# Where the weight sums are issued, and which tiles come last, in a two-block fp32 trunk on one core

## The chip, the core and the metric

The kernel runs on one core of a Trainium2 chip. The metric is device time in microseconds (us), from the first to the last instruction of one launch with a small overhead around it. The kernel before was timed three times: 2754.55 us median, 2754.36 to 2760.89.

## The reference, cut to what matters

A trunk of two blocks over 512 positions of width 2048, all in fp32. The first block has two layers. Each is a normalisation, an input product, two kinds of attention with gates, and an output product that is added to x:

```
for l in range(DEPTH):                     # DEPTH = 2
    h = rmsnorm(x, attn_norm_g[l])
    proj = h @ w_in[l]
    ...                                    # ya: windowed attention, yb: latent attention, both gated
    x = x + jnp.concatenate([ya, yb], axis=-1) @ w_out[l]
x = rmsnorm(x, final_norm_g)
```

The second block puts 16 meta tokens in front, and is one layer more of that form (with stick-breaking attention and a pooling branch), with its own normalisation ahead of it and one behind it:

```
zin = h @ w_in                             # h = rmsnorm_2(hs, gain)
...
merged = sigmoid(m_attn) * (o_attn @ w_attn_up) + sigmoid(m_pool) * (o_pool @ w_pool_up)
hs = hs + merged @ w_out
```

## The kernel before

Everything is kept transposed: a tile is 128 features by 512 positions, and a tensor of width 2048 is 16 such tiles. Every fp32 operand is split into a high and a low part (ScalarE casts the high part, `...h`; VectorE subtracts it from the source, `...l`), and one product is three TensorE matmuls (high by high, low by high, high by low).

Weights come through `next_w` (L253): it takes the next entry of the list `wq`, lets SyncE (SP) load 128x1024 numbers into `wr` (three buffers), lets ScalarE cast `wh` and VectorE subtract `wl` (three buffers each), and stays two entries ahead of TensorE. A *plain* output tile takes two entries and 48 matmuls of 512 columns. A *pair* of output tiles is made in the manner of Strassen and Winograd (`run_pair`, L346): seven products of 8 x 3 matmuls of 256 columns, 168 in all, over combinations of activations (`t_set`, tiles `t12`, `t34`) and of weights (`pair_steps`, L229). Two of the weight combinations of a pair are sums of blocks of the weight matrix. They are not made on an engine but by DMA: GpSimd (POOL) issues a copy of a block into a tensor `wsd` in HBM and then a DMA that adds another block to it (`sum_step`, L224; four such DMAs per pair, 48 pairs, 192 DMAs). `next_w` issues one at three of every four weight loads, from the start of the kernel until they are used up, each held until the TensorE instruction that was last issued at that point has ended (`behind_pe`). From `wsd` SP loads them as `ws` and `wr`, and VectorE adds a further block to `ws`.

In each layer of the first block the work is, in order: the input products with attention as side work, and then the output products ("output stage"): plain tiles 0 to 3, five pairs (tiles 4 to 13), plain tiles 14 and 15. Each output tile is added to the old x (`xo`, loaded by SP), stored (`xd<-xo`, SP), squared by ScalarE (`xq`), and the square is added up by GpSimd in `SumSq` (L445). In the second layer a copy scaled with the gain of the last normalisation (`xg`) is squared and added up as well (`xgq`). The next stage's activations are the new x times a gain, stored by ScalarE as `hrd` (or `xrd`) and read back by SP as `rr` tiles, which are split into `hh` and `hl`: rows 0 to 7 in the program under plain tile 14, rows 8 to 13 under plain tile 15; tiles 14 and 15 are split from on-chip data (`raw`). `scales` then splits the summed squares (`csh`) and TensorE sums them over the partitions (`csum`).

TensorE's order is as written; side work (attention heads, `t_build`, `scales`) is put between its products by an estimated clock. Every engine and every DMA queue runs its own list in order, so that a DMA on SP's list that waits holds all behind it.

In the second block, `o_load` (L1264) reads back a tile of the pooling branch (`ol`) and splits it (`o0h` ... `o7h`); four are issued before the last `ga` product and four behind it (`PRE`). `au_loads` (L1261) loads two tiles for each product of `au`.

Of the kernel before, what the change touches and what calls it, by code (L numbers as in the profile page):

```python
# [15 lines left out]
ALU = mybir.AluOpType  # L16
# [3 lines left out]
S = 512  # L20
NB = S // P
DM = 2048
NC = DM // P
# [15 lines left out]
NSLOT = 76  # L39
M2 = NM // 2  # L40
GPLAIN = 6
PRE = 4
EARLYT = 4
HEADS = {("ga", 0): 0, ("ga", 2): 1, ("ga", 4): 2, ("ga", 6): 3, ("pu", 1): 4, ("pu", 3): 5, ("pu", 5): 6, ("pu", 7): 7}
HN = S // 2
NPLAIN = 4
NSPILL = 8
SUMPAIRS = 48
NSIDE = 3
TP_WAIT = 4000  # L50

# [53 lines left out]
def trunk_kernel(ctx, tc, xT, w_in, w_qkv, w_out, w_in2, w_pool, w_aup, w_pup, w_out2, metaT, vec, cst, outT):  # L105
    nc = tc.nc
# [8 lines left out]
    def slot(name, dt=F32, cols=S):  # L115
        t = slots.tile([P, W], dt, tag="s", name=name)
        return t[:, :cols]
# [79 lines left out]
    def load_w_dma():  # L197
        src, n = wq.popleft()
        return w_raw(src, n), n

    wsd = tc.dram_tile([SUMPAIRS, 2, P, WCOLS + 16], F32, name="wsd")[:, :, :, :WCOLS]
    presum = deque()
    last_pe = [None, 0]

    def plan_sums(pairs):


        assert len(pairs) <= SUMPAIRS
        for p in range(0, len(pairs), 2):
# [6 lines left out]
                ops += [(wsd[k, 0], a22, 1), (wsd[k, 1], a11, 1)]  # L216
            presum.extend(ops)

    def behind_pe(ins):

        tc.add_manual_dep(ins.ins, last_pe[0].name, mybir.DependencyInfo(
            mybir.DependencyClass.Sync, mybir.DependencyReason.DATA), reason="pace")

    def sum_step():  # L224
        dst, src, add = presum.popleft()
        kw = {"accum_op": ALU.add} if add else {}
        behind_pe(nc.gpsimd.dma_start(dst, src, **kw))  # L227

    def pair_steps(p, a11, a12, a21, a22, n):  # L229

# [15 lines left out]
    def load_w_split(raw, n):  # L246
        hi = wp.tile([P, WCOLS], F32R, tag="wh", name="wh")[:, :n]
        lo = wp.tile([P, WCOLS], F32R, tag="wl", name="wl")[:, :n]
        nc.scalar.copy(hi, raw)  # L249
        tt(lo, raw, f32(hi), ALU.subtract)  # L250
        wready.append((hi, lo))

    def next_w():  # L253
        while len(wready) < 2 and wq:
            if callable(wq[0][0]):
                make, n = wq.popleft()
                load_w_split(make(), n)
            else:
                load_w_split(*load_w_dma())
            last_pe[1] += 1  # L260
            if last_pe[1] > 12 and last_pe[1] % 4 and presum:
                sum_step()
        return wready.popleft()

    def gemm(nt, nu, nk, rhs, wide=False, cols=S):
# [40 lines left out]
    def tick():  # L306
        for e in side[:NSIDE]:
            if e[1] <= clock[0]:
                step(e)
# [7 lines left out]
    def run_gemm(nu, nk, rhs, wide=False, group=1, n=S):  # L317
        g = gemm(group, nu, nk, rhs, wide, n)
        while True:
            try:  # L320
                next(g)
            except StopIteration as e:
                return e.value if wide or group > 1 else e.value[0]
            tick()
# [65 lines left out]
    def load(src, name, n=S, queue=nc.sync):  # L390
        t = slot(name, F32, n)
        queue.dma_start(t, src)
        return t
# [49 lines left out]
        return ps  # L443

    class SumSq:  # L445
        def __init__(self, name, cols=S):
            self.acc = None
            self.name = name
            self.cols = cols

        def add(self, x, n=None):
            q = slot(self.name + "q", F32, self.cols)
            act(q, x, AF.Square)
            if self.acc is None:
                self.acc = q
            else:
                nc.gpsimd.tensor_tensor(self.acc, self.acc, q, ALU.add)

    def gate_sigmoid(g, name):
        a = slot(name + "a")  # L460
# [285 lines left out]
    def plan():  # L746
        pairs = []
        for lay in range(DEPTH):
            t = 0
            for kind, i in SEQ1:  # L750
                if kind == "pa":
                    wq.append((w_qkv[lay, i, :, 0:1024], 1024))
                elif kind == "pb":
                    wq.append((w_qkv[lay, i, :, 1024:1664], 640))
                elif kind == "pc":
                    wq.append((w_qkv[lay, i, :, 1664:2176], 512))
                elif kind == "cq":
                    if i == 0:
                        grouped(w_in[lay], 0, GRP)
                    t += 1  # L760
                else:
                    for u in range(2):
                        wq.append((w_in[lay, t, u], WCOLS))
                    t += 1
            grouped(w_out[lay], 0, GRP)
            w = w_out[lay]
            for j in range(GRP, NPLAIN):
                for u in range(2):
                    wq.append((w[j, u], WCOLS))
            for j in range(NPLAIN, NC - 2, 2):  # L770
                blocks = (w[j, 0], w[j, 1], w[j + 1, 0], w[j + 1, 1])
                wq.extend(pair_steps(len(pairs), *blocks, WCOLS))
                pairs.append(blocks)
            for j in range(NC - 2, NC):
                for u in range(2):
                    wq.append((w[j, u], WCOLS))
        t = 0
        for kind, i in SEQ2:
            if kind == "pw":
                wq.append((w_pool[i], 512))  # L780
            elif kind == "au":
                wq.append((w_aup[i], WCOLS))
            elif kind == "pu":
                wq.append((w_pup[i], WCOLS))
            elif not _plain(kind, i):
                if i % 2 == 0:
                    blocks = (w_in2[t, 0], w_in2[t, 1], w_in2[t + 1, 0], w_in2[t + 1, 1])
                    wq.extend(pair_steps(len(pairs), *blocks, WCOLS))
                    pairs.append(blocks)
                t += 1  # L790
            else:
                for u in range(2):
                    wq.append((w_in2[t, u], WCOLS))
                t += 1
        grouped(w_out2, 0, GRP)
        for j in range(GRP, NPLAIN):
            for u in range(2):
                wq.append((w_out2[j, u], WCOLS))
        for j in range(NPLAIN, NC - 2, 2):
            blocks = (w_out2[j, 0], w_out2[j, 1], w_out2[j + 1, 0], w_out2[j + 1, 1])  # L800
            wq.extend(pair_steps(len(pairs), *blocks, WCOLS))
            pairs.append(blocks)
        for j in [NC - 2, NC - 1] * 2:
            for u in range(2):
                wq.append((w_out2[j, u], WCOLS))
        plan_sums(pairs)

    plan()

    k2 = {}  # L810
# [14 lines left out]
    def layer(lay, h, rd, x_src, x_dst):  # L825
# [62 lines left out]
            elif kind == "ga":  # L888
                gate["a", i] = gate_silu(run_gemm(2, 8, hget), rd["r"], "ga")

        sq = SumSq("x")
        if lay == 1:
            sq2 = SumSq("xg")
        res = [None] * NC
        rawd, w = (hrd, S) if lay == 0 else (xrd, W)

# [26 lines left out]
        def plain_out(j, ps):  # L923
            xo = xos.pop(j)
            tt(xo, ps, xo, ALU.add)
            tile_done(j, xo)
# [6 lines left out]
            xo_load(j)  # L933
            plain_out(j, run_gemm(2, 8, yget))
        need(lambda: len(ts) == 8)
        for j in range(NPLAIN, NC - 2, 2):
            xo_load(j)
            xo_load(j + 1)
            c = run_pair(ts, 8)
            t0, t1 = xos.pop(j), xos.pop(j + 1)  # L940
            add_pair(c, t0, t1)
            tile_done(j, t0)
            tile_done(j + 1, t1)
        c = t0 = t1 = None
        ts = None
        for j in range(NC - 2, NC):
            xo_load(j)
            for k in (range(8) if j == NC - 2 else range(8, NC - 2)):
                res[k] = split(load(rawd[:, k, :], "rr", w), "h", w)
            plain_out(j, run_gemm(2, 8, yget))  # L950
        if lay == 0:
            load_consts1()

# [74 lines left out]
    def scale0():  # L1028
        acc = squares[0]
        for n in range(1, NC):  # L1030
            ins = nc.vector.tensor_tensor(acc, acc, squares[n], ALU.add)
            if n == 1:
                behind_pe(ins)
        squares.clear()
        parts = split(acc, "cs")
        yield 19000
        r = slot("r")
        rsqrt_of(r, colsum(parts), 1.0 / DM, S)
        rd["r"] = r
# [221 lines left out]
    def au_loads(i):  # L1261
        return load(sgd[:, i, :], "sgl"), load(ypd[:, i, :], "ypl")
# [5 lines left out]
    for kind, i in SEQ2:  # L1268
# [19 lines left out]
                nc.gpsimd.dma_start(opd[:, 2 * i + d, :], t)  # L1288
        elif kind == "pu":
            gp = load(sgd[:, NC + i, :], "sgl", queue=nc.scalar)  # L1290
            yp = slot("yp")
            tt(yp, run_gemm(1, 8, lambda c: op[c]), gp, ALU.mult)
            nc.gpsimd.dma_start(ypd[:, i, :], yp)
        elif kind == "au":
            if i == 0:
                op = None
                need(lambda: all(t is not None for t in oa))
                tset = []
                ahead = {0: au_loads(0)}
            if i + 1 < NC:  # L1300
                ahead[i + 1] = au_loads(i + 1)
            ga, yp = ahead.pop(i)
# [13 lines left out]
        elif kind == "ga":  # L1316
            if i == 0:
                tset = None
            if i == SB - 1:
                for c in range(PRE):  # L1320
                    o_load(c)
            nc.gpsimd.dma_start(gad[:, i, :], gate_silu(run_gemm(2, 8, x2), sr, "ga"))
            if i == SB - 1:
                X2 = None
                for c in range(PRE, 8):
                    o_load(c)
        elif i % 2 == 0:
# [3 lines left out]
            for d, t in enumerate(c):  # L1331
# [7 lines left out]
                else:  # L1339
                    at = i + d + (0 if kind == "ma" else NC)  # L1340
# [39 lines left out]
    for j in range(NPLAIN):  # L1380
# [3 lines left out]
        q = finish(j, first[j] if j < GRP else run_gemm(2, 8, mget), full, S)  # L1384
# [151 lines left out]
```

## Time and profile before

| | |
|---|---|
| median of three runs | 2754.55 us (2754.36 to 2760.89) |
| profiled execution, its own time | 2764.74 us |
| its span | 2762.8 us |
| TensorE clock, mean of the span | 0.972 of full |
| busy: TensorE, VectorE, ScalarE, GpSimd | 95%, 70%, 50%, 19% |
| DMA bytes by queue: SP's and ScalarE's list (q1), GpSimd's (q0) | 328.89 MB, 128.66 MB |

The stages in the trace: start up to 62 us; input stage of layer 0 up to 528; its output stage up to 742; input stage of layer 1 up to 1252; its output stage up to 1470; then the second block up to 2762.8. A row of the trace names the engine, the line of the kernel, the operation and the tiles as out<-in. Times within a stage are read from the table by windows, where PE is TensorE, DVE is VectorE, ACT is ScalarE, POOL is GpSimd; "PEclk" is the granted share of TensorE's full clock, and "DMA share" the mean busy share of the 16 DMA engines.

### The profile page before, as it was taken

The page shows a single profiled execution, that of the slowest core. Times are in us where ns is not written, and L with a number is a line of the kernel's source. Part 1 is how long each engine was busy: PE and PEld are TensorE (multiplying, and loading weights), DVE is VectorE, ACT ScalarE, POOL GpSimd, SP SyncE. Part 2 cuts the span into 40 slices and gives each one's busy share as a digit, 9 for nine tenths or more (in the row PEclk, how much of TensorE's full clock was granted, in tenths as well). Part 3 has the DMA queues.
Part 4 walks back from the last instruction along what each step waited for, and adds up shares of the span by engine and source line. Part 5 has one row for each costly group of instructions (what it writes and reads, how often), then busy time and mean ns, then how long its engine had stood idle before and what let it go on. Part 6 is the DMA issues. An engine that isn't in the chain of part 4 may idle for free.

```text
span 2762.8 us, 41611 instructions
## 1 busy us (share of the span) xinstructions
PE 2631.1 (95%) x15961; PEld 2335.1 (85%) x15961; DVE 1925.3 (70%) x2923; ACT 1389.0 (50%) x2279; POOL 535.4 (19%) x564
## 2 busy tenths in 40 slices
PE   8999999989799999998978999999999998999997
PEld 6888888788588888887966999999999986878797
DVE  7767667776367657767857778777777755675686
ACT  5445455544335445554545544335565666643353
POOL 0121233222121213232431214000000022210012
PEclk9999999999899999999988999999999998999998
DMA  5455544689664555467986754544545543566555
GB/s 182 130 149 145 140 142 137 207 250 309 210 159 134 142 153 141 130 184 223 319 255 214 217 172 157 173 154 154 167 150 170 174 131 119 174 208 209 191 172 183
DMA packets 168055, 492.52 MB, mean 178 GB/s; under 512 B 19233, under 2 KB 23841, under 8 KB 167857
## 3 DMA queue, kind: packets, MB, share of 16 engines
q1 hardware_dynamic: 113936, 328.89, 35.8%
q0 software_dynamic: 36208, 128.66, 18.9%
q10 hardware_dynamic: 17712, 32.32, 3.3%
q8 instruction: 125, 2.05, 0.3%
q14 instruction: 74, 0.60, 0.1%
HBM read 428.19 MB, written 162.27 MB: 214 GB/s over the span
## 4 chain that ended last, share of the span: by engine, by line
PE 45%; DMA 3%; DVE 3%; ACT 1%; issue 1%; POOL 0%; SPq 0%; ACTq 0%; DVEq 0%; POOLq 0%
PE mm L160 13%; PE y L160 13%; PE x L160 9%; PE z L160 8%; DMA xd<-xo 1%; DMA rr<-xrd 1%; DVE wl L129 1%; PE zB L160 1%; DVE out L1414 0%; PE so L160 0%; PE pw L160 0%; PE zA L160 0%; ACT wh L249 0%; DMA xo<-xd 0%; DMA vr<-vd 0%
## 5 line engine op out<-in xcount | busy, mean ns | idle before, releaser
L249 ACT CAST wh<-wr 128x1024 fp32r<-128x1024 f32 (+2 forms) x448 | 462.2, 1032 | 556.0 <-PE mm L160 241.9
L129 DVE TENSOR_TENSOR wl<-wr,wh 128x1024 fp32r<-128x1024 f32 (+2 forms) x448 | 564.3, 1264 | 226.8 <-ACT wh L249 212.9
L160 PE MATMUL mm<-hh,wh 128*128 128x512 f32 x1248 | 504.2, 404 | 30.2 <-ACT hh L151 23.3
L160 PE MATMUL mm<-hl,wh 128*128 128x512 f32 x1248 | 497.3, 398 | 1.4 <-DVE hl L129 0.9
L160 PE MATMUL mm<-hh,wl 128*128 128x512 f32 x1248 | 496.1, 397 | 0.6 <-DVE wl L129 0.5
L160 PEld LDWEIGHTS mm<-hh,wh 128*128 128x128 f32 x1248 | 237.6, 190 | 79.7 <-ACT hh L151 27.0
L160 PEld LDWEIGHTS mm<-hh,wl 128*128 128x128 f32 x1248 | 237.2, 190 | 56.5 <-DVE wl L129 1.7
L160 PEld LDWEIGHTS mm<-hl,wh 128*128 128x128 f32 x1248 | 237.5, 190 | 51.3 <-DVE hl L129 5.1
L249 ACT CAST wh<-ws 128x1024 fp32r<-128x1024 f32 x144 | 151.3, 1051 | 182.8 <-PE y L160 128.3
L160 PE MATMUL y<-t34h,wh 128*128 128x256 f32 (+1 forms) x768 | 217.7, 283 | 2.8 <-DVE ab L129 2.7
L160 PE MATMUL y<-t34l,wh 128*128 128x256 f32 (+1 forms) x768 | 217.1, 283 | 0.0
L160 PE MATMUL y<-t34h,wl 128*128 128x256 f32 (+1 forms) x768 | 216.5, 282 | 0.0
L129 DVE TENSOR_TENSOR wl<-ws,wh 128x1024 fp32r<-128x1024 f32 x144 | 179.3, 1245 | 24.1 <-ACT wh L249 21.3
L227 POOL DMA_DIRECT2D wsd<-in_w_in x132 | 90.8, 690 | 450.1 <-PE mm L160 219.7
L160 PE MATMUL x<-hh,wh 128*128 128x256 f32 (+1 forms) x528 | 148.9, 282 | 0.0
L160 PE MATMUL x<-hl,wh 128*128 128x256 f32 (+1 forms) x528 | 148.7, 282 | 0.0
L160 PE MATMUL x<-hh,wl 128*128 128x256 f32 (+1 forms) x528 | 148.6, 281 | 0.0
L160 PEld LDWEIGHTS y<-t34h,wh 128*128 128x128 f32 x768 | 145.3, 189 | 3.2 <-issue 3.2
L160 PEld LDWEIGHTS y<-t34l,wh 128*128 128x128 f32 x768 | 145.7, 190 | 0.0
L160 PEld LDWEIGHTS y<-t34h,wl 128*128 128x128 f32 x768 | 145.4, 189 | 0.0
L129 DVE TENSOR_TENSOR ws<-ws,wr 128x1024 f32<-128x1024 f32 x96 | 136.2, 1419 | 3.2 <-DMA wr<-in_w_out 0.2
L160 PE MATMUL z<-t12h,wh 128*128 128x256 f32 (+1 forms) x384 | 109.7, 286 | 17.8 <-ACT t12h L151 17.8
(1171 smaller groups left out, 6801.0 us busy)
## 6 DMA issues: line engine op xcount, KB each, us to landing
wr<-in_w_in SPq DMA_DIRECT2D x255, 512.0 KB, 3.9
wsd<-in_w_in POOLq DMA_DIRECT2D x132, 512.0 KB, 6.7
wr<-in_w_out SPq DMA_DIRECT2D x85, 512.0 KB, 5.3
wsd<-in_w_out POOLq DMA_DIRECT2D x60, 512.0 KB, 5.7
ws<-wsd SPq DMA_DIRECT2D x48, 512.0 KB, 4.4
wr<-wsd SPq DMA_DIRECT2D x48, 512.0 KB, 4.2
tr<-yd SPq DMA_DIRECT2D x32, 256.0 KB, 5.9
xd<-xo SPq DMA_DIRECT2D x32, 256.0 KB, 6.1
```

Source lines behind the costliest of these rows:

```text
L129: nc.vector.tensor_tensor(out, a, b, op)
L160: last_pe[0] = nc.tensor.matmul(out, a, b, start=start, stop=stop, skip_group_check=True).ins
L227: behind_pe(nc.gpsimd.dma_start(dst, src, **kw))
L249: nc.scalar.copy(hi, raw)
```

## The change

There are five edits. (1) `hold` keeps `next_w` from issuing weight sums from the start of an output stage of the first block until its last plain tile; elsewhere it issues three sums per two loads instead of three per four, each held behind a TensorE instruction three loads older (`marks[0]`). (2) The added squares `xq` and `xgq` of these stages go to VectorE. (3) Each output stage of the first block has four pairs (tiles 4 to 11) and then four plain tiles (12 to 15), with four, four, four and two rows read back under them; there are 46 pairs with sums in all. (4) All eight `o_load`s stand ahead of the last `ga` product. (5) `au_loads(0)` moves ahead of the last `pu` product. The delay of `scale0` is changed too (19000 to 23000); the order of TensorE's work is the same for it.

```diff
-PRE = 4
+PRE = 8
-SUMPAIRS = 48
+SUMPAIRS = 46
...
+    hold = [0]
+    marks = deque(maxlen=4)
...
-    def behind_pe(ins):
+    def behind_pe(ins, at=None):
-        tc.add_manual_dep(ins.ins, last_pe[0].name, mybir.DependencyInfo(
+        tc.add_manual_dep(ins.ins, (at or last_pe[0]).name, mybir.DependencyInfo(
...
-        behind_pe(nc.gpsimd.dma_start(dst, src, **kw))
+        behind_pe(nc.gpsimd.dma_start(dst, src, **kw), marks[0])
...
             last_pe[1] += 1
-            if last_pe[1] > 12 and last_pe[1] % 4 and presum:
+            marks.append(last_pe[0])
+            if last_pe[1] > 12 and hold[0] == 0 and presum:
                 sum_step()
+                if last_pe[1] % 2 and presum:
+                    sum_step()
...
-                nc.gpsimd.tensor_tensor(self.acc, self.acc, q, ALU.add)
+                self.eng.tensor_tensor(self.acc, self.acc, q, ALU.add)
...
-        sq = SumSq("x")
+        hold[0] = 1
+        sq = SumSq("x", eng=nc.vector)
         if lay == 1:
-            sq2 = SumSq("xg")
+            sq2 = SumSq("xg", eng=nc.vector)
...
-        for j in range(NPLAIN, NC - 2, 2):
+        for j in range(NPLAIN, NC - 4, 2):
             xo_load(j)
             xo_load(j + 1)
             c = run_pair(ts, 8)
...
-        for j in range(NC - 2, NC):
+        for j in range(NC - 4, NC):
             xo_load(j)
-            for k in (range(8) if j == NC - 2 else range(8, NC - 2)):
+            for k in range((j - NC + 4) * 4, min((j - NC + 5) * 4, NC - 2)):
                 res[k] = split(load(rawd[:, k, :], "rr", w), "h", w)
             plain_out(j, run_gemm(2, 8, yget))
+        hold[0] = 0
...
             gp = load(sgd[:, NC + i, :], "sgl", queue=nc.scalar)
+            if i == NC - 1:
+                ahead = {0: au_loads(0)}
```

GpSimd's list in the output stage of layer 0 (`wsd` is a weight sum, `xq` the added squares; `gag` and `ya` are a gate and an attention result of the stage ahead, `cqnsq` belongs to the stage behind). Before:

```order
L227 DMA wsd<-in_w_in 128x1024
L457 TENSOR_TENSOR xq<-xq 128x512
L227 DMA wsd<-in_w_in 128x1024 x5
L457 TENSOR_TENSOR xq<-xq 128x512 x2
L227 DMA wsd<-in_w_in 128x1024 x5
L457 TENSOR_TENSOR xq<-xq 128x512
```

Now, from the last gate of the input stage to the first work of the next one:

```order
L481 TENSOR_TENSOR gag<-gag,gaa 128x512
L612 TENSOR_TENSOR ya<-ya,gag 128x512
L850 DMA yd_91<-ya 128x512
L229 DMA wsd<-in_w_in 128x1024 x15
L463 TENSOR_TENSOR cqnsq<-cqnsq 128x512 x2
```

Sums and squares are gone from GpSimd's list between the last `yd` store and the next stage; sums begin again when its weights are loaded. Per stage the list now has 93 sums in the input stage of layer 0 and 91 in that of layer 1, and none later; before it had 48, 36 (output), 57, 35 (output) and 16 (second block).

SP's list at the end of the output stage of layer 0 (`wr` weights of the next stage, `rr` rows read back, `xo` the old x of tile 15, `xd` the store of a new x). Before:

```order
L194 DMA wr_6801<-in_w_in 128x1024
L392 DMA rr_6471<-hrd_90 128x512
L392 DMA rr_6477<-hrd_90 128x512
L194 DMA wr_6832<-in_w_in 128x1024
L392 DMA rr_6483<-hrd_90 128x512
L392 DMA xo_6563<-in_xT 128x512
L392 DMA rr_6565<-hrd_90 128x512
L194 DMA wr_6863<-in_w_in 128x1024
L899 DMA xd0_93<-xo_6563 128x512
L392 DMA rr_6571<-hrd_90 128x512
```

Now:

```order
L194 DMA wr_6715<-in_w_in 128x1024
L397 DMA rr_6415<-hrd_90 128x512
L397 DMA rr_6421<-hrd_90 128x512
L194 DMA wr_6746<-in_w_in 128x1024
L397 DMA xo_6499<-in_xT 128x512
L397 DMA rr_6501<-hrd_90 128x512
L194 DMA wr_6778<-in_w_in 128x1024
L906 DMA xd0_93<-xo_6499 128x512
L397 DMA rr_6507<-hrd_90 128x512
```

The load of the old x for tile 15 stands at the same place among the weights of the next stage; behind it two rows are still to be read back, one of them behind the store, where five more stood before.

ScalarE's list in the second block before the `au` products (`o4h` to `o7h` are the casts of pooling tiles; `vh`, `sp`, `sph` belong to the attention head that TensorE's `zA` waits for). Before:

```order
L151 CAST o3h<-ol 128x512
L151 CAST vh<-vt 128x512
L136 ACTIVATE sp<-zA 128x512
L136 ACTIVATE sp<-zB 128x512
L136 ACTIVATE sp<-sp 128x512 x4
```

Now:

```order
L151 CAST o3h<-ol 128x512
L151 CAST o4h<-ol 128x512
L151 CAST o5h<-ol 128x512
L151 CAST o6h<-ol 128x512
L151 CAST o7h<-ol 128x512
L151 CAST vh<-vt 128x512
L136 ACTIVATE sp<-zA 128x512
```

Four casts, each of which waits for its load, now stand ahead of the head's chain.

## Rows read from the trace of the kernel before

**Rows 1.** Table by windows: input and output stages of both layers
```profile
core 0: us, PE busy (x) PEld busy (x) DVE busy (x) ACT busy (x) POOL busy (x), PEclk, DMA share, GB/s
62.00:528.00 466.00, 465.56 (x2367) 391.42 (x2366) 318.03 (x614) 239.28 (x485) 110.44 (x108) 1.00 0.51 144
528.00:742.00 214.00, 172.80 (x1099) 154.17 (x1098) 132.60 (x176) 92.73 (x128) 49.61 (x53) 0.90 0.87 271
742.00:1252.00 510.00, 509.59 (x2543) 426.74 (x2544) 339.34 (x643) 254.39 (x505) 122.59 (x121) 0.99 0.53 147
1252.00:1470.00 218.00, 175.65 (x1094) 156.01 (x1093) 148.49 (x185) 102.04 (x157) 74.61 (x65) 0.88 0.85 261
```

**Rows 2.** TensorE's waits, output stage of layer 0: total, times, longest us
```profile
PE csum L160 <- ACT csh L151: 13.0, 1, 13.0
PE z L160 <- ACT t12h L151: 9.2, 2, 5.1
PE z L160 <- DVE wl L129: 6.2, 2, 4.6
PE mm L160 <- ACT hh L151: 5.2, 3, 3.6
PE mm L160 <- ACT y12h L151: 2.9, 1, 2.9
```

**Rows 3.** The same waits, output stage of layer 1
```profile
PE mm L160 <- ACT hh L151: 18.0, 3, 10.6
PE z L160 <- ACT t12h L151: 8.6, 2, 7.1
```

**Rows 4.** Table by windows: pair stretches and ends of both output stages
```profile
581.00:662.00 81.00, 74.82 (x610) 74.40 (x610) 52.54 (x62) 36.63 (x46) 22.25 (x25) 0.96 0.96 289
711.00:743.00 32.00, 12.80 (x38) 7.22 (x38) 14.74 (x20) 14.62 (x23) 3.55 (x4) 0.71 0.71 248
1300.00:1356.00 56.00, 54.94 (x458) 54.52 (x457) 44.16 (x53) 29.03 (x40) 24.38 (x22) 0.99 0.97 288
1356.00:1404.00 48.00, 41.61 (x324) 41.02 (x323) 33.66 (x39) 22.44 (x33) 20.68 (x18) 0.93 1.01 321
1428.00:1468.00 40.00, 16.53 (x42) 9.61 (x40) 17.94 (x23) 16.79 (x28) 7.12 (x6) 0.62 0.60 181
```

**Rows 5.** DMA, output stage of layer 0: GpSimd's queue, and its sums
```profile
q0 software_dynamic: 5264, 19.14, 36.7%
...
wsd<-in_w_in POOLq DMA_DIRECT2D x36, 512.0 KB, 7.7
```

**Rows 6.** DMA, input stage of layer 0: GpSimd's queue, and weight loads
```profile
q0 software_dynamic: 8112, 29.10, 27.0%
...
wr<-in_w_in SPq DMA_DIRECT2D x52, 512.0 KB, 4.1
```

**Rows 7.** Timeline, end of layer 0's output stage: start, us, engine, line, op
```profile
711.05 0.39 PE L160 MATMUL mm<-y15l,wh 128*128 128x512 f32 x1
...
711.28 0.39 PE L160 MATMUL mm<-y15h,wl 128*128 128x512 f32 x1
...
718.98 0.38 SPq L392 DMA_DIRECT2D xo<-in_xT  x1
...
735.68 3.30 ACT L151 CAST hh<-rr 128x512 fp32r<-128x512 f32 x5 [6.78 <-DMA rr<-hrd]
```

**Rows 8.** VectorE's weight add and scaled copy, by tile: ns min/median/max
```profile
L129 DVE TENSOR_TENSOR ws<-ws,wr x96: 1212/1226/2217, 557.8 to 2702.4; 128x1024 f32<-128x1024 f32 x96
...
L906 DVE TENSOR_SCALAR xg<-xo,vecs x16: 479/1515/1579, 1265.6 to 1462.7; 128x512 f32<-128x512 f32 x16
```

**Rows 9.** GpSimd's added squares, by lines: busy us, mean ns, idle before
```profile
L457 POOL TENSOR_TENSOR xq<-xq 128x512 f32<-128x512 f32 x30 | 49.9, 1664 | 89.7 <-ACT xq L136 89.7
```

**Rows 10.** Timeline, second block before the `au` products
```profile
2324.13 1.74 SPq L392 DMA_DIRECT2D ol<-opd  x4
...
2327.47 0.79 PE L160 MATMUL zA<-sph,tri 128*128 128x512 f32 x1 [4.58 <-ACT sph L151]
```

More of the change, by code (lines that the diff above doesn't have):

```diff
@@ L445, in trunk_kernel, with __init__ @@
     class SumSq:
-        def __init__(self, name, cols=S):
+        def __init__(self, name, cols=S, eng=nc.gpsimd):
             self.acc = None
+            self.eng = eng
             self.name = name
@@ L935, in layer @@
         need(lambda: len(ts) == 8)
-        for j in range(NPLAIN, NC - 2, 2):
+        for j in range(NPLAIN, NC - 4, 2):
             xo_load(j)
@@ L945, in layer @@
         ts = None
-        for j in range(NC - 2, NC):
+        for j in range(NC - 4, NC):
             xo_load(j)
-            for k in (range(8) if j == NC - 2 else range(8, NC - 2)):
+            for k in range((j - NC + 4) * 4, min((j - NC + 5) * 4, NC - 2)):
                 res[k] = split(load(rawd[:, k, :], "rr", w), "h", w)
             plain_out(j, run_gemm(2, 8, yget))
+        hold[0] = 0
         if lay == 0:
@@ L1035, in scale0 @@
         parts = split(acc, "cs")
-        yield 19000
+        yield 23000
         r = slot("r")
@@ L1298, in trunk_kernel @@
                 tset = []
-                ahead = {0: au_loads(0)}
             if i + 1 < NC:
```

## The prediction, made before the changed kernel ran

> **What bounds the kernel now.** I read the table by windows first, cut at the stage borders, to see where TensorE isn't busy. In the two input stages it lacks almost nothing: 465.56 of 466 us and 509.59 of 510, at a DMA share of 0.51 and 0.53. In the two output stages it lacks 41.2 of 214 us and 42.4 of 218, the granted clock falls to 0.90 and 0.88, and the DMA share is 0.87 and 0.85 [rows 1]. So nearly all that can be won in the first block lies in 432 us.
>
> The list of TensorE's waits says for what it waits there: in layer 0 13.0 us for `csh` (the summed squares), 9.2 for `t12h`, 6.2 for `wl`, 5.2 for `hh` (rows read back) [rows 2]; in layer 1 18.0 for `hh` and 8.6 for `t12h` [rows 3]. ScalarE and VectorE are named, but neither is full; they wait for loads: five `hh` casts come after 6.78 us of ScalarE's idleness that a DMA ended [rows 7].
>
> A finer table by windows separates two kinds of loss. In the pairs the DMA share is 0.96 to 1.01 and TensorE loses some: 81 against 74.82, 48 against 41.61, with the clock at 0.96 and 0.93. At the end of each stage it loses most: 12.80 of 32 us busy at clock 0.71, and 16.53 of 40 at 0.62 [rows 4]. In matmuls: one of 512 columns follows the last at 0.23 us (711.05 to 711.28) [rows 7], so the 38 of the first end are worth 8.7 us and the 42 of the second 9.7. Lost are 23.3 and 30.3 us, of which some is the half clock into which TensorE falls once it has stood still.
>
> **The sums and the DMA engines.** GpSimd's queue takes 36.7% of the DMA time of layer 0's output stage [rows 5], 78.5 of 214 us; nearly all of it is 36 sums, so one costs 2.18 us of all 16 engines. Without them the share there is 0.87 - 0.37 = 0.50, that of an input stage today. Layer 1's output stage has 35. Thus every load of the stage is faster, and each wait above that ends with a load shrinks.
>
> *Pairs:* idle time and lost clock come to (81 - 74.82) + 0.04 x 81 = 9.4 us in layer 0, and (56 - 54.94) + 0.01 x 56 = 1.6 and (48 - 41.61) + 0.07 x 48 = 9.8 in layer 1 [rows 4]: 20.8 together. Nothing but the full DMA engines explains it, but the 56 us stretch shows that a share of 0.97 alone costs little. I take -17; ends 0 and -21.
>
> *Start of the stages:* the waits for `t12h` are 9.2 and 8.6 us, the longest of the kind for `y12h` 2.9 [rows 2, 3]. They end with a chain (attention result, store, read back, four VectorE operations, split) of which the DMA is a part. I take -4 and -1.5; ends 0 and -21.
>
> *Input stages:* they get 45 and 34 sums more. 45 x 2.18 = 98 us lift the share of layer 0's from 0.51 to 0.72, 34 x 2.18 = 74 us that of layer 1's from 0.53 to 0.68. The cover is the three weight buffers: a load of weights is issued some 3 x 24 x 0.23 = 16.6 us less a cast and a subtraction (some 2.4) before its use, 14 us, and takes 4.1 [rows 6]. A sum took 7.7 us to land even at 0.87 [rows 5]. So I take +2; ends 0 and, at the loss of the worst stretch (9.4 of 81 us) over all 976 us, +113.
>
> The Trainium skill, "DMA: Bandwidth & Descriptors", section "Issuing engines are not separate DMA queues", speaks against the move: DMAs of all issuing engines end up on the same 16 engines and interleave, so a sum that is issued elsewhere is charged elsewhere. The trace agrees that queues share (the weight loads slow with the share); by that rule alone the gain of the pairs would turn up as a loss in the input stages, which is the slower rival below.
>
> **The ends of the stages.** Now 14 rows are read back under the last two plain tiles, eight under the first, so that most arrive after the last tile is done; TensorE then waits row by row (`hh`), and SP's list is held by weight loads whose buffers aren't free. The load of the old x for tile 15 goes out at 718.98, 7.7 us after the last matmul of that tile [rows 7]; and five more rows stand behind the store that needs it. With four rows under each of four tiles, 12 of 14 are there when tile 15 starts. But on SP's list `xo` of tile 15 still stands behind the same weight loads. With E as the end of the last plain tile: the buffer that the load ahead of `xo` needs is free at E + 2.4, `xo` lands 5 us later (between 4.1 and 7.7 [rows 5, 6]), the addition 0.65, the store and the next issue 1, the last row's load 5, then four operations (cast, square, added square, cast) of 0.66 each (3.30 for five [rows 7]): `csum` at about E + 16.7, its window 18 us instead of 32. That is -14. In layer 1 `xo` stands one weight load later on SP's list (24 x 0.23 = 5.5), and `xg` adds some 1.5: 25 instead of 40, -15. Sum -29; ends 0 (if the order on SP's list is all that counts) and -53.6, all that is lost.
>
> **Two plain tiles for a pair.** 96 matmuls of 0.23 us are 22.1 us; 168 of 256 columns at 54.94/458 = 0.120 [rows 4] are 20.2. Twice +1.9 is +4, certain within 1.
>
> **Squares on VectorE.** GpSimd makes 30 `xq` additions [rows 9]; layer 1 has 15 more for `xg`. On VectorE one is half the size of the 1.21 us `ws` addition, so some 0.65: 29 us in both stages. Against it: the `ws` addition takes 1.21 us at its best and 2.22 at its worst, `xg` 0.48 and 1.52 (median 1.515) [rows 8]; if the slow cases are those beside GpSimd's additions, 16 `ws` and 16 `xg` give back 1.0 each, 32. VectorE is at 44.16 of 56 us in the pairs of layer 1 [rows 4], so there is room either way. I take 0; ends -4 and +10, should the additions stand ahead of the `wl` that the next pair waits for.
>
> The Trainium skill, "SBUF — State Buffer", section "Who interferes with whom", says that a VectorE instruction with two SBUF inputs contends with a GpSimd instruction that reads SBUF, and that the second blocks fully. The two levels of the `ws` row agree. By this rule the edit gives the -3 above; without it VectorE would be 29 us busier, the rival below.
>
> **`o_load`s and `au_loads`.** The four later `ol` loads are issued from 2324.13 to 2325.87 [rows 10]; they wait for free tiles, which the change does not free earlier. At 4.1 us they land at 2330, and `vh` with the chain to `zA` now stands behind the cast of the last. `zA`, for which TensorE waits 4.58 us already, starts at 2327.47 [rows 10]; behind o7h's cast (2330.6) and the chain's own 4.5 us it would start near 2335, +7.7. Four casts of 0.66 are out of the way later, so +5; ends 0 (if the tiles come free earlier) and +8. `au_loads(0)` puts two loads on SP's list earlier: +1; ends 0 and +2.
>
> **The sum** is -17 - 4 - 1.5 + 2 - 29 + 4 + 0 + 5 + 1 = -39.5 us. The profiled execution took 2764.74 us, 10 above the median; the sum would make it 2725. I apply it to the median, 2754.55: 2715 us, with 2698 to 2732 as the likeliest case's own range.
>
> **Rivals.**
> - *Nearly all the loss goes:* faster loads end the stalls before the clock falls, which takes away the half clock as well. The two ends give -53, the pairs -21, half of `t12h` -9, less +9 for the other edits: -74, 2680. For it: in the input stages TensorE lacks under half a microsecond at a share of 0.51, the share that the output stages will have. Against it: SP's list, which holds `xo` of tile 15.
> - *The ends stay:* the wait is set by the order on SP's list and not by the rows, and only some -10 of the -29 come: 2734. For it: `xo` has not moved against the weights. Against it: its weight load waits for TensorE, which no longer waits for rows.
> - *VectorE becomes the bound in the pairs:* the additions cost 29 us and nothing is given back: 2744. Against it: the free and the slow `ws` addition [rows 8].
> - *The input stages fill the DMA engines (slower):* sums come in twos, weights are late, and half the loss rate of the worst stretch (5.8%) holds for 976 us: +57, 2772. It decides once a weight load takes over 14 us from issue to landing; it takes 4.1 now. Against it: 0.72 is far below 0.96.
> - *The change does not do what it says:* the output stages stay full because their own loads fill what the sums leave, 2755. Against it: the share left is 0.50.
>
> **How the numbers follow.** The forecast has 58%, the rival with the whole gain 14, the ends that stay 14, VectorE 6, the full input stages 6, no effect 2. To tell a change from none takes 0.3%, 8 us. Faster than 2746: the first three, and half of VectorE's: 88 to 89%, put at 0.88. Within 8 us: no effect and the rest of VectorE's, 0.05. Slower: 0.07, where the full input stages and a `zA` chain worse than priced lie. The range goes from 2687, into the first rival, to 2744, past the second: a little under 2 in 10 lies outside.
>
> **What would show it.** After the change the windows of the output stages should show a DMA share near 0.5 and a clock above 0.95 in the pairs; the input stages 0.68 to 0.72 with TensorE still within 2 us of full; the time from the last plain tile to `csum` near 17 and 24 us; no `ws` addition above 1.3 us in the output stages; `zA` of the last head waiting some 5 us more. The prediction is wrong if TensorE's waits for `wl` or `wh` show up in an input stage, or if the ends still take over 28 us.

## The result, and the profile after

The changed kernel takes 2714.46 us (median of four runs, 2707.63 to 2715.73) against 2756.6 in the runs beside it: a ratio of 0.984, 95% interval 0.9819 to 0.9862. It is faster by 42 us (44 by the ratio). The profiled execution took 2714.61 us, its span is 2712.5.

The table by windows, cut at the stages as they lie now (columns as in [rows 1]):

```profile
62.00:528.00 466.00, 465.86 (x2370) 391.91 (x2369) 324.68 (x621) 242.64 (x488) 141.68 (x155) 1.00 0.72 196
528.00:717.00 189.00, 166.79 (x1028) 148.99 (x1026) 123.47 (x173) 86.45 (x120) 5.56 (x8) 0.94 0.69 223
717.00:1224.00 507.00, 506.91 (x2536) 424.82 (x2537) 342.11 (x641) 254.45 (x502) 134.31 (x147) 1.00 0.64 175
1224.00:1413.00 189.00, 166.67 (x1025) 148.06 (x1023) 135.90 (x202) 99.62 (x152) 0.00 (x0) 0.94 0.61 201
```

The output stages are 25 and 29 us shorter, at a DMA share of 0.69 and 0.61 where it was 0.87 and 0.85. The input stages carry the sums now, at 0.72 and 0.64, and TensorE loses 0.1 us in either. Not all sums are gone from layer 0's output stage. Eight of the 15 that GpSimd's list has behind the last `yd` store go out there, the first at 677.04 us, 16 us ahead of the last plain tile's end: `next_w` is two loads ahead, and each sum is held only behind a TensorE instruction three loads older. From the DMA view of 528 to 717 us:

```profile
wsd<-in_w_in POOLq DMA_DIRECT2D x8, 512.0 KB, 6.6
```

GpSimd's queue has 9.1% of the DMA time of that window, for 36.7% before [rows 5]. The finer windows that answer to [rows 4]:

```profile
571.00:652.00 81.00, 81.00 (x659) 80.42 (x659) 60.34 (x78) 40.18 (x52) 0.00 (x0) 0.98 0.63 201
1268.00:1349.00 81.00, 81.00 (x664) 80.36 (x664) 65.85 (x93) 45.57 (x65) 0.00 (x0) 0.98 0.63 201
...
692.00:717.00 25.00, 9.84 (x41) 7.39 (x39) 11.98 (x16) 10.62 (x17) 1.89 (x3) 0.75 0.87 288
1389.00:1413.00 24.00, 10.18 (x40) 7.08 (x38) 11.99 (x18) 11.60 (x20) 0.00 (x0) 0.75 0.58 202
```

In the pairs TensorE no longer stands still. At the ends it still does, for 15 of 25 and 14 of 24 us. TensorE's waits in the output stage of layer 0, then of layer 1 (answers to [rows 2, 3]):

```profile
PE csum L160 <- ACT csh L151: 15.2, 1, 15.2
PE z L160 <- ACT t12h L151: 3.9, 2, 2.3
PE mm L160 <- ACT y12h L151: 1.8, 1, 1.8
```

```profile
PE csum L160 <- ACT csh L151: 12.9, 1, 12.9
PE z L160 <- ACT t12h L151: 6.0, 2, 4.4
```

The waits for `wl` and, nearly, for `hh` are gone; that for `csh` is now the longest in both stages, as it was before in layer 0 alone. To see what each stage gave, I took from every trace the start of the same matmuls of TensorE and formed the stretches between them (us). "Start" is from the first output product to the first pair's product (`z<-t12h`), "tiles" from there to the last plain tile's last matmul, "end" from there to `csum`:

| stretch | before | after | difference |
|---|---|---|---|
| up to layer 0's output stage | 511.5 | 511.2 | -0.3 |
| layer 0: start | 55.1 | 49.1 | -6.0 |
| layer 0: tiles | 144.7 | 132.7 | -12.0 |
| layer 0: end | 30.8 | 23.2 | -7.6 |
| layer 1: input stage | 490.9 | 490.2 | -0.7 |
| layer 1: start | 50.9 | 50.5 | -0.4 |
| layer 1: tiles | 145.4 | 132.9 | -12.5 |
| layer 1: end | 38.0 | 22.4 | -15.6 |
| second block up to the pooling products (`o0h`) | 854.0 | 855.5 | +1.5 |
| from there to the merged products (`mg0h`) | 252.9 | 257.0 | +4.1 |
| from there to the end | 188.5 | 187.9 | -0.6 |

They add up to -50 us, the difference of the spans. The profiled execution of before is 8 us above the median of its runs, that of after is at its median.

### The profile page after: what moved, and what is told of

It reads as the page before. It is cut to its first block, busy times and chain, and to the rows that moved or that the text cites. A ratio compares the mean times of both kernels' runs of the same rounds, so it can differ in the third digit from the quotient of the medians.

```text
span 2712.5 us, 41183 instructions
## 1 busy us (share of the span) xinstructions
PE 2615.1 (96%) x15817; PEld 2321.9 (86%) x15817; DVE 1914.1 (71%) x2944; ACT 1383.3 (51%) x2269; POOL 449.9 (17%) x511
## 4 chain that ended last, share of the span: by engine, by line
PE 90%; DVE 4%; DMA 2%; ACT 2%; issue 1%; POOL 0%; SPq 0%; ACTq 0%; DVEq 0%; POOLq 0%
PE mm L160 43%; PE y L160 15%; PE x L160 10%; PE z L160 10%; PE msc L160 2%; PE qn L160 1%; PE mo L160 1%; PE sc L160 1%; PE o L160 1%; PE tp L164 1%; PE kn L160 1%; DVE wl L129 1%; PE v L160 1%; DMA rr<-hrd 1%; PE mtp L164 1%
## 5 line engine op out<-in xcount | busy, mean ns | idle before, releaser
L251 ACT CAST wh<-ws 128x1024 fp32r<-128x1024 f32 x138 | 144.9, 1050 | 180.3 <-PE y L160 123.4
L160 PE MATMUL y<-t34h,wl 128*128 128x256 f32 (+1 forms) x736 | 207.6, 282 | 0.0
L160 PE MATMUL y<-t34l,wh 128*128 128x256 f32 (+1 forms) x736 | 207.4, 282 | 0.0
L160 PE MATMUL y<-t34h,wh 128*128 128x256 f32 (+1 forms) x736 | 207.0, 281 | 0.1
L129 DVE TENSOR_TENSOR wl<-ws,wh 128x1024 fp32r<-128x1024 f32 x138 | 172.0, 1246 | 24.1 <-ACT wh L251 21.5
L160 PEld LDWEIGHTS y<-t34h,wh 128*128 128x128 f32 x736 | 138.4, 188 | 0.2 <-issue 0.2
L160 PEld LDWEIGHTS y<-t34l,wh 128*128 128x128 f32 x736 | 138.4, 188 | 0.0
L160 PEld LDWEIGHTS y<-t34h,wl 128*128 128x128 f32 x736 | 138.3, 188 | 0.0
L129 DVE TENSOR_TENSOR ws<-ws,wr 128x1024 f32<-128x1024 f32 x92 | 120.5, 1310 | 2.6
L160 PE MATMUL z<-t12h,wh 128*128 128x256 f32 (+1 forms) x368 | 104.2, 283 | 9.9 <-ACT t12h L151 9.9
## 6 DMA issues: line engine op xcount, KB each, us to landing
tr<-yd SPq DMA_DIRECT2D x32, 256.0 KB, 4.0
xd<-xo SPq DMA_DIRECT2D x32, 256.0 KB, 2.6
```

Source lines behind the costliest of these rows:

```text
L129: nc.vector.tensor_tensor(out, a, b, op)
L160: last_pe[0] = nc.tensor.matmul(out, a, b, start=start, stop=stop, skip_group_check=True).ins
```

## The experiments

Each kernel was timed beside the kernel before on the same chip; ratios are to that, and a gain in us is the ratio's distance from 1 (or from the changed kernel's 0.984) times 2758 us, about the time of the kernel before beside them. The first ones make one edit alone.

**The kernel before, traced a second time.**

> The kernel before once more, unchanged, for a second trace of it. The first profiled execution took 2764.74 us, 8 above the median of the timed runs (2756.6). Theory: the excess lies in the output stages, whose loads meet full DMA engines by chance of timing, so a second trace at 2754 to 2760 us shows shorter waits there (ends of the stages or pairs) and input stages within 1 us of the first. Rival: the excess is spread evenly or lies in the second block, then the output stages agree within 2 us.

It took 2759.68 us. Its stretches agree with the first trace within 1.3 us but for layer 0's tiles (141.4 for 144.7) and the part of the second block before the merged products (248.7 for 252.9). So some 3 us of the excess lay in layer 0's pairs and 4 in the second block: neither theory as put. In layer 0's pairs the DMA share is 0.96 [rows 4], but in that part of the second block it is 0.55, so that full DMA engines do not account for all of the scatter. No difference of a single stretch under 4 us is read as an effect below, unless it repeats.

**Edit 1 alone: the sums held and moved.**

```diff
-        behind_pe(nc.gpsimd.dma_start(dst, src, **kw))
+        behind_pe(nc.gpsimd.dma_start(dst, src, **kw), marks[0])
...
-            if last_pe[1] > 12 and last_pe[1] % 4 and presum:
+            marks.append(last_pe[0])
+            if last_pe[1] > 12 and hold[0] == 0 and presum:
                 sum_step()
+                if last_pe[1] % 2 and presum:
+                    sum_step()
...
+        hold[0] = 1
         sq = SumSq("x")
...
+        hold[0] = 0
```

> The kernel before with edit 1 alone (no weight sums under the output products, three per two loads elsewhere, held behind older matmuls). Theory (the sums' DMA time is the main cause): 25 to 35 us faster; the last plain tile of layer 0 ends 15 to 20 us earlier, the pairs lose under 3 us per layer, the ends shrink from 31 and 38 us to 20 to 28. Rival (the order of tiles and rows is the main cause): under 15 us faster, the ends stay at 28 us or more.

Ratio 0.9883 [0.9862, 0.9905], 32 us faster. Layer 0's start and tiles shrink to 49.1 and 130.8 us, layer 1's tiles to 136.6. But layer 0's end stays at 31.1, and layer 1's falls only to 32.3. The pairs of layer 0 and both ends in its windows:

```profile
581.00:662.00 81.00, 81.00 (x687) 81.00 (x686) 62.78 (x74) 42.24 (x53) 12.68 (x8) 1.00 0.65 210
690.00:723.00 33.00, 13.83 (x41) 8.82 (x40) 14.16 (x19) 14.00 (x22) 4.10 (x5) 0.72 0.74 259
1400.00:1433.00 33.00, 13.84 (x37) 8.05 (x35) 14.64 (x18) 14.57 (x25) 5.51 (x4) 0.62 0.46 161
```

TensorE is busy for all 81 us at full clock where 6.2 us and 4% of the clock were missing. Layer 1's end is 32 us long at a DMA share of 0.46: free DMA engines take it from 38.0 us to that and no further. The theory holds for the time and the pairs and fails for the ends, which it put at 20 to 28 us.

**Edit 3 alone: four plain tiles, four rows under each.**

```diff
-        for j in range(NPLAIN, NC - 2, 2):
+        for j in range(NPLAIN, NC - 4, 2):
...
-        for j in range(NC - 2, NC):
+        for j in range(NC - 4, NC):
...
-            for k in (range(8) if j == NC - 2 else range(8, NC - 2)):
+            for k in range((j - NC + 4) * 4, min((j - NC + 5) * 4, NC - 2)):
```

> The kernel before with edit 3 alone (four pairs and four plain tiles, four rows read back under each). Theory (sums first): 5 to 15 us faster, as the ends shrink to 20 to 25 us but the pairs still lose 7 to 10 us per layer beside the sums, and the plain tiles cost 4. Rival (order first): 25 us or more faster.

Ratio 0.9957 [0.9944, 0.9969], 12 us faster. Its ends are 24.9 and 32.4 us, 5.9 and 5.6 shorter; the tiles are within 2.2 of before. Layer 1's end was to be 20 to 25 and is not: edit 1 alone and edit 3 alone each leave it at 32; together they make it 22.4 (22.3 without edit 2, in the run further below).

**Edit 2 alone: the squares on VectorE.**

```diff
-                nc.gpsimd.tensor_tensor(self.acc, self.acc, q, ALU.add)
+                self.eng.tensor_tensor(self.acc, self.acc, q, ALU.add)
...
-        sq = SumSq("x")
+        sq = SumSq("x", eng=nc.vector)
...
-            sq2 = SumSq("xg")
+            sq2 = SumSq("xg", eng=nc.vector)
```

> The kernel before with edit 2 alone (added squares of the output stages on VectorE). Theory: no change within 5 us; every addition to ws and every xg in the output stages falls to 1.2 and 0.48 us. Rival (GpSimd's additions, which slow VectorE, cause the waits for wl in the pairs): 10 to 20 us faster. Rival (VectorE becomes the bound): 5 to 20 us slower.

Ratio 1.0018 [1.0006, 1.0029], 5 us slower. Inside, it is two effects of opposite sign: layer 0's tiles 137.5 us (-7.2), layer 1's 155.1 (+9.7). Against the second trace of the kernel before they are -3.9 and +8.9, so that only layer 1's loss is an effect by the measure above. VectorE's weight additions are free in both. Here is the row of `ws` in layer 1's pairs:

```profile
L129 DVE TENSOR_TENSOR ws<-ws,wr x8: 1218/1223/1226, 1305.2 to 1387.8; 128x1024 f32<-128x1024 f32 x8
```

Yet layer 1's pairs wait for weights. Among ScalarE's waits from 1300 to 1434 us of this run is one that neither trace of the kernel before has there:

```profile
ACT m L363 <- DMA xd<-xo: 12.2, 4, 4.5
```

`m` is ScalarE's copy of a pair's product. It waits for stores of finished tiles, since it takes the place of a tile that is still being stored, and the cast of the next weights stands behind it on ScalarE's list (TensorE's waits for `wh` in those pairs come to 11.6 us). VectorE is at 41.15 of 56 us, so it is not the bound. My reading is that beside full DMA engines a faster VectorE only brought the wait for stores forward; it rests on the waits of one trace, and no run tried it.

**The changed kernel with the squares back on GpSimd.**

```diff
-        sq = SumSq("x", eng=nc.vector)
+        sq = SumSq("x")
...
-            sq2 = SumSq("xg", eng=nc.vector)
+            sq2 = SumSq("xg")
```

> The changed kernel with the added squares back on GpSimd (edit 2 undone). In the kernel before, edit 2 alone made the pairs of layer 0 7 us shorter and those of layer 1 10 us longer. Theory: with the sums gone it matters less: layer 0 within 3 us either way, layer 1 2 to 5 us shorter, and the ends 1 to 3 us longer by the slower additions on GpSimd; total within 4 us. Rival (VectorE is the bound of layer 1's pairs): layer 1 shorter by 8 us or more. Rival (the shared slowdown is what counts): both layers longer by 5 us or more.

Ratio 0.985 [0.9833, 0.9866], 3 us slower than the changed kernel by the ratios, which is not clear of the intervals. Layer 0's tiles are the same (133.0), layer 1's 138.9 for 132.9. The total is as expected, but layer 1 went the other way: it was to be 2 to 5 us shorter with the squares on GpSimd and is 6 longer. With the sums gone, the same edit that cost 10 us in layer 1 gains 6. What is left is the slowdown of VectorE beside GpSimd's additions, in the row of `xg`; that this makes the 6 us is argued and not shown. This run's `xg` row beside that of the changed kernel:

```profile
L913 DVE TENSOR_SCALAR xg<-xo,vecs x16: 481/1511/1594, 1237.4 to 1413.3; 128x512 f32<-128x512 f32 x16
```

```profile
L913 DVE TENSOR_SCALAR xg<-xo,vecs x16: 477/481/490, 1238.5 to 1408.5; 128x512 f32<-128x512 f32 x16
```

**The changed kernel without edits 4 and 5.**

```diff
-PRE = 8
+PRE = 4
...
-            if i == NC - 1:
-                ahead = {0: au_loads(0)}
...
                 tset = []
+                ahead = {0: au_loads(0)}
```

> The changed kernel with edits 4 and 5 undone (four o_loads before the last ga product and four behind it, au_loads(0) at its old place). Theory: 4 to 7 us faster than the changed kernel, and the wait of zA for sph falls from 11.9 to some 5 us; the time between the first pooling product and the first merged product falls from 257 to 250 to 253. Rival (these edits cost nothing, the second block varies by itself): within 2 us of the changed kernel.

2709.57 us, ratio 0.9818 [0.9804, 0.9833], about 6 us faster than the changed kernel; the stretch before the merged products is 250.5 for 257.0. In the changed kernel's timeline one sees the late loads, the casts behind them and the head's chain:

```profile
2270.32 1.33 SPq L397 DMA_DIRECT2D ol<-opd  x3
...
2274.06 0.62 ACT L151 CAST o5h<-ol 128x512 fp32r<-128x512 f32 x1 [4.42 <-DMA ol<-opd]
...
2276.45 0.58 ACT L151 CAST vh<-vt 128x512 fp32r<-128x512 f32 x1
...
2281.00 0.79 PE L160 MATMUL zA<-sph,tri 128*128 128x512 f32 x1 [11.88 <-ACT sph L151]
```

ScalarE stands 4.42 us before `o5h`, and `vh` behind `o7h`; `zA` waits 11.88 us for what took 4.58 before [rows 10]; in this run it is 4.4. The stretch repeats: 256.0 to 259.5 us in the four other traces of the changed kernel's variants that keep edits 4 and 5, 249.6 to 251.3 in the three without them.

**The sums held six weight loads longer.**

```diff
+            hold[1] -= 1
+            if hold[1] == 0:
+                hold[0] = 0
...
-        hold[0] = 0
+        hold[1] = 6
```

> The changed kernel with the weight sums held for six more weight loads after the last plain tile. In layer 0 sums resume in the last microseconds of the end, where the DMA share is above 0.9 and the load of the old x of tile 15 takes 9.3 us. Theory: that load lands in 5 us, the end of layer 0 shrinks from 23.2 to 17 to 19 us, layer 1 (no sums left) stays within 1 us; 4 to 6 us faster. Rival (the order on SP's list alone sets it): layer 0's end within 2 us.

2706.66 us, ratio 0.9809 [0.979, 0.9828]. Layer 0's end is 18.1 us for 23.2, layer 1's 21.9, and the load of the old x of tile 15 lands in 3.7 us: as expected. The total is 8 us faster by the ratios, above the 4 to 6 expected, but its interval overlaps that of the changed kernel. Sums that come back with the next stage's first weight loads, which `next_w` makes two loads ahead of TensorE, fall into layer 0's end; here the first goes out at 719.73 us, behind `csum`.

**The old x of tile 15 loaded with that of tile 14.**

```diff
-            xo_load(j)
+            if j not in xos:
+                xo_load(j)
+            if j == NC - 2:
+                xo_load(j + 1)
```

> The changed kernel with the old x of tile 15 loaded together with that of tile 14, so that it no longer stands behind the weights of the next stage on SP's list. Theory (that load and what follows it set csum): csum 6 to 10 us sooner after the last plain tile in each layer, 23.2 to 13 to 17 and 22.4 to 13 to 16; 10 to 18 us faster in all. Rival (the last rows read back set it, behind the same weights): under 3 us per layer.

2716.15 us, ratio 0.9842 [0.9828, 0.9857]: nothing. The ends are 24.8 and 21.9 us. My theory of the ends, which the prediction used too, has fallen as the only cause, and the time is the rival's. The timeline of layer 1's end shows what sets it now:

```profile
1392.14 0.69 DVE L129 TENSOR_TENSOR xo<-mm,xo 128x512 f32<-128x512 f32 x1 [2.31 <-PE mm L160]
...
1399.83 0.33 SPq L194 DMA_DIRECT2D wr<-in_w_in  x1
...
1400.21 1.37 SPq L397 DMA_DIRECT2D rr<-xrd  x3
...
1403.92 0.63 ACT L151 CAST hh<-rr 128x528 fp32r<-128x528 f32 x1 [3.68 <-DMA rr<-xrd]
1404.46 0.62 ACT L136 ACTIVATE xq<-xo 128x512 f32<-128x512 f32 x1
...
1409.17 0.62 ACT L136 ACTIVATE xq<-xo 128x512 f32<-128x512 f32 x1
```

Tile 15 is added at 1392.14, right after its last matmul; its square comes at 1409.17, 17 us later. ScalarE's list has the casts of the rows ahead of it, and even the square of tile 14 (1404.46) stands behind a row that SP issues only at 1400.21, behind a weight load. In the changed kernel itself the addition comes late as well:

```profile
1402.56 0.68 DVE L129 TENSOR_TENSOR xo<-mm,xo 128x512 f32<-128x512 f32 x1
...
1407.20 0.63 ACT L151 CAST hh<-rr 128x528 fp32r<-128x528 f32 x1 [3.91 <-DMA rr<-xrd]
1407.74 0.62 ACT L136 ACTIVATE xq<-xo 128x512 f32<-128x512 f32 x1
```

There the old x, issued at 1398.22, lands at 1401.98 and the addition follows; its square then stands behind a row cast. Taking the first delay away leaves the second.

**Rows split after the tile's square.** On top of the last edit:

```diff
-                res[k] = split(load(rawd[:, k, :], "rr", w), "h", w)
+                res[k] = load(rawd[:, k, :], "rr", w)
             plain_out(j, run_gemm(2, 8, yget))
+            for k in range((j - NC + 4) * 4, min((j - NC + 5) * 4, NC - 2)):
+                res[k] = split(res[k], "h", w)
```

> The changed kernel with the old x of tile 15 loaded with that of tile 14, and each of the four plain tiles' rows split only after the tile itself is added and squared, so that ScalarE's squares no longer stand behind casts that wait for rows. The run with the early old x alone left the ends at 24.8 and 21.9 us; its trace shows the square of tile 15 17 us after its sum, behind row casts. Theory (ScalarE's in-order list behind rows that stand behind weights on SP's list sets csum): ends of 13 to 17 us in layer 1 and 16 to 20 in layer 0 (where sums still run), 8 to 15 us faster than the changed kernel. Rival (the DMA time of the rows themselves sets it): ends within 2 us of 23.2 and 22.4, or as much waiting moved to hh.

2690.49 us, ratio 0.9749 [0.9734, 0.9765], 24 us faster than the changed kernel (25 by the ratios) and more than expected: the ends are 14.7 and 7.9 us. TensorE works without a pause through the 7.9 us, so nothing is left to win there. The new order also lets SP issue the rows earlier, ahead of weights. Layer 1's end:

```profile
1382.39 0.69 DVE L129 TENSOR_TENSOR xo<-mm,xo 128x512 f32<-128x512 f32 x1 [2.25 <-PE mm L160]
...
1383.12 0.63 ACT L136 ACTIVATE xq<-xo 128x512 f32<-128x512 f32 x1
...
1386.04 1.16 ACT L151 CAST hh<-rr 128x528 fp32r<-128x528 f32 x2
...
1389.87 0.39 PE L160 MATMUL csum<-csh,ones_r 128*128 128x512 f32 x1
```

The square follows the addition by 0.7 us, and `csum` runs at full clock (0.39 us; 0.79 in the changed kernel) with no wait in front of it. This run changes two things against the one before it, the casts' place and through it SP's order; which of them gives how much was not tried apart. Nor were the casts moved without the early old x: against the changed kernel the 24 us belong to both edits together, of which the early old x alone gives nothing.

**The combinations.** The first has the diffs of the run without edits 4 and 5 and of the longer hold:

> The changed kernel with edits 4 and 5 undone and the sums held six weight loads longer: the two single edits gave -5 and -8 us (of which 5 in the end of layer 0). If they are independent, 10 to 12 us faster than the changed kernel, 2702 to 2705 us. Rival: they share what they give back, under 7 us.

2703.1 us, ratio 0.9795 [0.978, 0.981]: independent, as expected. The second has the early old x and the later split as well:

> Both together: edits 4 and 5 undone, sums held longer, old x of tile 15 early, rows split after the squares. Theory: the ends of both stages at 12 to 16 us, 2685 to 2695 us. Rival (ends don't move): 2702 to 2705 us.

2679.27 us (five runs, 2678.08 to 2682.22), ratio 0.9712 [0.9696, 0.9727]: 79 us faster than the kernel before and 35 faster than the changed one. The ends are 10.0 and 7.9 us and the time is some 6 us better than the best expected, both below their ranges. It beats both kernels.

## Why the prediction was right, and where its terms were off

The time, 2715 us, and the direction came true. That it did to half a microsecond is luck: the sum behind it has two terms that erred against each other, and it was taken from spans and applied to a median. Against the spans it was -39.5 us where the traces have -50; the medians, which leave out the 8 us by which the traced run of before was slow, have -42.

*The sums' DMA time, right in the input stages.* 45 and 34 sums more were to lift the input stages to 0.72 and 0.68; they show 0.72 and 0.64, and TensorE loses no more there (+2 expected, -1 measured). Layer 1's share is below the forecast because eight of its sums already ran in the output stage ahead of it. That the DMA engines are shared, whichever engine issues, is what the Trainium skill says ("DMA: Bandwidth & Descriptors", "Issuing engines are not separate DMA queues"). The trace agrees: the weight loads of layer 0's input stage land in 6.1 us (median) where it was 4.1 [rows 6]. The slower rival that I built on it did not come: the slowest lands in 11.5 us, within the 14 us of slack that I had estimated, and TensorE has no wait for weights in either input stage. The output stages keep 0.69 and 0.61, not 0.5. The bytes that are not sums move in a shorter stage, which turns 0.50 into some 0.57 (0.50 x 214 / 189, an estimate from [rows 1] and [rows 5]), and in layer 0 the eight sums add 0.09; the rest, 0.03 there and some 0.06 in layer 1, is open.

*Start of the stages, right in the sum:* -5.5 expected, -6.4 measured, nearly all of it in layer 0.

*Pairs and plain tiles, too small:* -17 + 4 = -13 expected, -24.5 measured. The term counted losses in 185 us of windows only; what follows them up to the last plain tile (in layer 0 the 49 us from 662) was left out of it, and it kept back a fifth. The run with edit 1 alone shows -13.9 and -8.8 from the sums in the two layers. The price of the plain tiles was right: with the sums gone, layer 0's tiles take 130.8 us with five pairs and 132.7 with four.

*The ends, too large, and with the wrong mechanism:* -29 expected, -23.2 measured. Windows of 18 and 25 us were forecast, that is some 17 and 24 to `csum`; they are 23.2 and 22.4. The step that failed is the chain behind "`xo` lands": I let the old x of tile 15 set it alone and gave the row casts on ScalarE's list no more than their own time. Loading it early changed nothing, and moving the casts behind the squares as well took 8.5 and 14.5 us from the changed kernel's ends. In layer 0 another 5 us are sums that come back too soon; the prediction held the sums to be gone there. The order of ScalarE's list, which I looked at in the second block, would have shown the first, and the 15 sums on GpSimd's list behind the last `yd` store the second.

*Squares on VectorE:* 0 expected. In the changed kernel they are worth some 3 us, which is not clear of the intervals, with 6 in layer 1's tiles. The give-back was right: `xg` takes 0.48 us throughout, and 1.51 in the median with the squares on GpSimd. The Trainium skill's rule ("SBUF — State Buffer", "Who interferes with whom") that VectorE and GpSimd block one another over SBUF agrees with that. What I had not seen is that alone, beside full DMA engines, the edit is 5 us slower, as it seems because what is gained on VectorE waits for stores. This is also why the single edits do not add up: -32, -12, +5 and +6 (edits 4 and 5) make -33 where the change gave -44 by the ratio, and edit 2 in company accounts for some 8 of the 11 missing.

*`o_load`s and `au_loads`, right:* +6 expected. The table has +5.6, but the +1.5 of it ahead of the pooling products is there without these edits too (855.7 us); what is theirs is the 6 us that the run without them gives back, 6.5 in its stretch; `zA` waits 7.3 us more where +7.7 was worked out.

## What to carry to other kernels

Where one stage has its DMA engines full and its neighbours have them half full, work that may run at any time belongs to the neighbours; the slack of a prefetch, from issue to use, tells whether they can take it (here 14 us, against loads that came to take up to 11.5). When the first wait goes, read the lists of the in-order engines at the place where the next one ends: here moving casts behind a square, with one load brought forward, gave 24 us, over half of what the whole change gave. Where one delay stands behind another, taking away the first shows nothing. An edit that frees an engine can lose time beside a full resource and gain it once that is relieved, so that edits are judged together as well as alone.

## What was not expected of the hardware

A DMA share of 0.63 to 0.72 costs TensorE nothing here (465.86 of 466 us busy at 0.72, 81.00 of 81 at 0.63). At 0.96 the loss in layer 0's pairs was 9.4 of 81 us, and it went with the sums; at 0.97 it was only 1.6 of 56 in layer 1. So a share near 1 does not by itself say what it costs. In the ends of the changed kernel the granted clock is 0.75 over 25 us, and `csum` takes 0.79 us there; in the run with the rows split after the squares the clock of layer 1's end stays at full and `csum` takes 0.39. The two ends became 23.0 us shorter by it where TensorE's two waits for `csh` lost 21 (15.2 and 12.9 us before, 6.7 and under 0.5 after). The 2 us more may be the clock, but they are below what I read as an effect.
